# Gated delta rule in a 256-token, four-layer forward pass: forward substitution on 16-row blocks instead of 32-row blocks, and the doubling steps woven by hand into the last gate projection

## The chip, the cores and the metric

One NeuronCore of a Trainium2 chip runs the whole program; the other cores are idle. The metric is the device time of one execution in microseconds (us), lower is better. The profile names the engines PE (TensorE matmuls), PEld (its weight loads), DVE (VectorE), ACT (ScalarE), POOL (GpSimd) and SP (SyncE, which here only issues DMAs).

## The reference

Four layers over 256 tokens of width 1024, all in fp32: MLA attention, MoBA attention, a gated-delta-rule (GDN) layer and a forgetting-attention (FoX) layer; the first two each carry an MLP. The change touches the GDN layer alone. Per head and per chunk of 64 tokens it solves a unit lower triangular system:

```
a_mat = jnp.where(strict, jnp.einsum('bhncd,bhnsd->bhncs', kb, kc) * decay, 0.0)
rhs = jnp.concatenate([vc * bc[..., None], kb * jnp.exp(gcum)[..., None]], axis=-1)
sol = lax.linalg.triangular_solve(a_mat, rhs, left_side=True, lower=True, unit_diagonal=True)
...
def step(S, inp):
    v_new = u_i - jnp.einsum('bhck,bhkv->bhcv', w_i, S)
    o = (jnp.einsum('bhck,bhkv->bhcv', q_i * jnp.exp(g_i)[..., None], S)
         + jnp.einsum('bhcs,bhsv->bhcv', attn_i, v_new))
    S = S * jnp.exp(g_last)[..., None, None] + jnp.einsum('bhck,bhcv->bhkv', k_dec, v_new)
...
o = rms_norm_2(o, o_norm) * jax.nn.silu(z.reshape(B, L, H, GDN_DV))
return o.reshape(B, L, W) @ w_out
```

## The kernel before

Activations live in SBUF with tokens or features on the 128 partitions. Matmuls that must keep fp32 accuracy are made of three fp32r products of split operands (`mm3`, lines 173 to 176: hi*hi, lo*hi, hi*lo); a weight tile of 128x1024 comes by a DMA on SP's queue into `raw`, is copied to `whi` on ScalarE (line 166) and its rest is formed as `wlo` on VectorE (line 167), each in a ring of four buffers. Small squares are multiplied as plain fp32. A scheduler orders the instructions of each engine from their order in the source, their dependencies and a planner's costs; `queued(after)` and `tc.issue_after` add an ordering by hand. PSUM has eight tiles of 128x512: four named `acc` and four named `aux`.

The GDN layer works in chunks of 128 tokens (two, `t`) for 8 heads: 16 units `u`, each with a 128x128 triangular matrix, kept transposed in `NT_`. Its stages, in the order of the source:

- projections with a short convolution for keys, queries and values, two heads at a time (`conv`, lines 930 to 944), each followed one step later by `keys`, `queries` or `values`. `values` (line 1064) transposes the values of a pair on TensorE; its pairs are named values(0) to values(3) below.
- `system`, after the last keys: the four 32x32 diagonal blocks of each of the 16 units go through DRAM (`n_d`) so that each of the 64 blocks lies on a partition of its own, in two halves (128 partitions). GpSimd inverts them by substitution: 31 steps of two elementwise instructions (lines 1008 and 1010).
- `spread`: the inverted blocks go through DRAM (`x_d`, line 1019) back to rows (line 1023), and `place` copies them on ScalarE (line 1030) into `X`, the block diagonal inverse. `spread_T` (line 1036) transposes `X` into `X[:, 1]`, four units (a quad) at a time.
- `grow`: two doubling steps, 32 to 64 and 64 to 128 rows. For each quad, `grow_a` (line 1074) multiplies `NT_` with `X` and VectorE masks the product into `t1`; `grow_b` (line 1089) multiplies `t1` with `X` (at 32 also its transposed twin) and VectorE subtracts (line 1091).
- `gate(1, ...)`: the second half of the output gate, 48 fp32r products of 512 columns between the last projections and the doubling. values(3) is placed between its halves (`between`).
- then `solve` (line 1153), `state`, `correct`, `output` and the output projection.

Of the kernel before, what the change touches and what calls it, by code (L numbers as in the profile page):

```python
# [10 lines left out]
F32 = mybir.dt.float32  # L11
# [47 lines left out]
def layout(inputs):  # L59
# [16 lines left out]
    for s in (32, 64):  # L76
        b = i // s
        cols[f"off{s}"] = ((b[:, None] == b[None, :] + 1) & (b[:, None] % 2 == 1)).astype(np.float64)
# [18 lines left out]
    eye = np.zeros((P, 32, 16), np.float32)  # L97
    for p in range(P):
        for c in range(16):
            eye[p, 2 * c + p // 64, c] = 1.0  # L100
# [10 lines left out]
def kernel(ctx: ExitStack, tc: tile.TileContext, I: dict, out: bass.AP, small_at: dict):  # L111
# [61 lines left out]
    def mm3(o, l, r, start, stop):  # L173
        T.matmul(o, lhsT=l[0], rhs=r[0], start=start, stop=False)  # L174
        T.matmul(o, lhsT=l[0], rhs=r[1], start=False, stop=False)  # L175
        T.matmul(o, lhsT=l[1], rhs=r[0], start=False, stop=stop)  # L176
# [123 lines left out]
    def proj_tok(hT, w, c0, n, between=None):  # L300
# [536 lines left out]
    def gdn():  # L837
# [25 lines left out]
        def gate(q4, h_T, scale, between=None):  # L863

            a = proj_tok(h_T, w, 3 * D + 512 * q4, 512, between)
            for t in range(NT):
# [6 lines left out]
                G.tensor_tensor(zs, zs, C["gdn_o_norm_2"][:, None, :].to_broadcast([P, 4, P]), op=ALU.mult)  # L873
# [52 lines left out]
        behind = []  # L926

        def conv(part, hp):
# [15 lines left out]
            behind[0:1] = [A.activation(dst, y, AF.Silu).ins]  # L944
# [397 lines left out]
```

## Time and profile before

| | |
|---|---|
| median of 3 runs | 953.02 us (951.78 to 958.95) |
| the profiled execution | 948.23 us |
| its span, first to last instruction | 946.4 us |
| mean granted TensorE clock | 0.988 |
| busy: PE / PEld / DVE / ACT / POOL | 95% / 80% / 69% / 56% / 15% |
| GDN layer's last products to its solve | 704.47 to 751.17 us |

In timeline rows the columns are: start, duration, engine, source line, operation, output<-inputs, shape, count, and in brackets the idle time of the engine just before and what ended it. An fp32 matmul of 128x128 has two records in such a row, a transpose one. Times of the profile are from the span's start.

### The profile page before, as it was taken

How to read it: one execution, taken by the hardware profiler on the slowest of the kernel's cores; microseconds unless marked ns; L12 is line 12 of the kernel's file. 1: busy time of each engine (PE TensorE's matmuls, PEld its weight loads, DVE VectorE, ACT ScalarE, POOL GpSimd, SP SyncE). 2: the span in 40 equal slices, each digit the busy share in tenths (PEclk: the TensorE clock that was granted, in tenths of full speed). 3: DMA queues.
4: the chain of work that ended last, by engine and by line, in shares of the span. 5: the costliest groups of instructions: out<-in, count | busy, mean ns of one | idle time of the engine just before them, and what ended most of it. 6: DMA issues, size and time to landing. Idle time of an engine off the chain costs nothing. (4 is left out here: it accounts for less than half of the span.)

```text
span 946.4 us, 13774 instructions
## 1 busy us (share of the span) xinstructions
PE 895.7 (95%) x4962; PEld 756.7 (80%) x4962; DVE 655.8 (69%) x1399; ACT 529.1 (56%) x1001; POOL 144.1 (15%) x190
## 2 busy tenths in 40 slices
PE   8899889999999999999999999999994998998995
PEld 7676678888888878777888888889994986887884
DVE  5997476767665666658566656679982788767775
ACT  6885365655554656555555445489654136755652
POOL 1121123233222100031000000010487000000000
PEclk9999999999999999999999999999997999999998
DMA  8546147777777854437666666355752115456331
GB/s 279 162 134 200 45 157 233 201 207 220 211 207 208 188 162 145 155 91 234 192 197 190 204 199 187 81 173 154 197 168 77 46 47 181 138 171 195 118 111 67
DMA packets 97300, 154.55 MB, mean 163 GB/s; under 512 B 10840, under 2 KB 65920, under 8 KB 96976
## 3 DMA queue, kind: packets, MB, share of 16 engines
q1 hardware_dynamic: 87072, 141.53, 47.8%
q0 software_dynamic: 10016, 12.11, 6.3%
q8 instruction: 39, 0.64, 0.3%
q14 instruction: 29, 0.24, 0.1%
q10 hardware_dynamic: 144, 0.03, 0.0%
HBM read 147.84 MB, written 5.78 MB: 162 GB/s over the span
## 5 line engine op out<-in xcount | busy, mean ns | idle before, releaser
L167 DVE TENSOR_TENSOR wlo<-raw,whi 128x1024 fp32r<-128x1024 f32 (+3 forms) x198 | 239.8, 1214 | 142.1 <-ACT whi L166 140.8
L166 ACT ACTIVATE whi<-raw 128x1024 fp32r<-128x1024 f32 (+3 forms) x202 | 205.9, 1025 | 151.4 <-DMA raw<-in_mlp_w_in_dram 79.6
L679 PE MATMUL aux<-s,whi 128*128 128x512 f32 x512 | 182.3, 399 | 2.7 <-DVE s L260 2.3
L174 PE MATMUL acc<-whi,s 128*128 128x512 f32 (+2 forms) x408 | 160.5, 398 | 5.0 <-ACT whi L166 2.4
L175 PE MATMUL acc<-wlo,s 128*128 128x512 f32 (+2 forms) x408 | 158.8, 391 | 0.8 <-DVE wlo L167 0.8
L176 PE MATMUL acc<-whi,s 128*128 128x512 f32 (+2 forms) x408 | 157.3, 387 | 0.0
L680 PE MATMUL aux<-s,wlo 128*128 128x256 f32 x512 | 143.9, 281 | 2.7 <-DVE wlo L167 2.7
L679 PEld LDWEIGHTS aux<-s,whi 128*128 128x128 f32 x512 | 96.2, 188 | 26.7 <-DVE s L260 2.8
L680 PEld LDWEIGHTS aux<-s,wlo 128*128 128x128 f32 x512 | 96.7, 189 | 4.5 <-DVE wlo L167 3.4
L174 PE MATMUL acc<-s,w2k 128*128 128x512 f32 x256 | 99.9, 390 | 0.0
L175 PE MATMUL acc<-s,w2k 128*128 128x512 f32 x256 | 99.8, 390 | 0.0
L176 PE MATMUL acc<-s,w2k 128*128 128x512 f32 x256 | 99.6, 389 | 0.0
L174 PEld LDWEIGHTS acc<-whi,s 128*128 128x128 f32 x408 | 76.5, 188 | 22.9 <-ACT whi L166 3.5
L175 PEld LDWEIGHTS acc<-wlo,s 128*128 128x128 f32 x408 | 76.8, 188 | 15.1 <-DVE wlo L167 3.1
L176 PEld LDWEIGHTS acc<-whi,s 128*128 128x128 f32 x408 | 76.9, 189 | 13.9 <-issue 0.3
L167 DVE TENSOR_TENSOR s<-raw,s 128x1024 fp32r<-128x1024 f32 x64 | 75.8, 1220 | 8.3 <-ACT s L166 8.1
L166 ACT ACTIVATE s<-raw 128x1024 fp32r<-128x1024 f32 x68 | 68.3, 1048 | 14.1 <-PE acc L176 6.8
L176 PE MATMUL acc<-s,wlo 128*128 128x256 f32 x256 | 72.6, 285 | 3.1 <-DVE wlo L167 3.1
L175 PE MATMUL acc<-s,whi 128*128 128x256 f32 x256 | 73.0, 286 | 0.5 <-DVE s L260 0.2
L174 PE MATMUL acc<-s,whi 128*128 128x256 f32 x256 | 72.9, 285 | 0.4 <-ACT s L259 0.2
L441 POOL DMA_DIRECT2D bias_d<-s x64 | 48.3, 969 | 130.0 <-ACT s L435 111.4
L176 PEld LDWEIGHTS acc<-s,w2k 128*128 128x128 f32 x256 | 48.1, 188 | 10.2
(365 smaller groups left out, 1423.7 us busy)
## 6 DMA issues: line engine op xcount, KB each, us to landing
raw<-in_mlp_w_in_dram SPq DMA_DIRECT2D x64, 512.0 KB, 5.2
raw<-in_mlp_w_out_dram SPq DMA_DIRECT2D x64, 512.0 KB, 3.9
raw<-in_gdn_w_in_dram SPq DMA_DIRECT2D x32, 512.0 KB, 4.4
raw<-in_moba_w_qkv_dram SPq DMA_DIRECT2D x24, 512.0 KB, 4.4
raw<-in_fox_w_in_dram SPq DMA_DIRECT2D x16, 512.0 KB, 5.0
raw<-in_kv_w_dram SPq DMA_DIRECT2D x16, 512.0 KB, 3.8
raw<-in_mla_w_o_dram SPq DMA_DIRECT2D x8, 512.0 KB, 3.6
bias_d<-s POOLq DMA_DIRECT2D x64, 64.0 KB, 4.7
```

Of the source, the lines that this page charges most:

```text
L166: i = A.activation(hi[:, :k * b], rs, AF.Copy)
L167: j = e.tensor_tensor(lo[:, :k * b], rs, hi[:, :k * b].bitcast(F32), op=ALU.subtract)
L174: T.matmul(o, lhsT=l[0], rhs=r[0], start=start, stop=False)
L175: T.matmul(o, lhsT=l[0], rhs=r[1], start=False, stop=False)
L176: T.matmul(o, lhsT=l[1], rhs=r[0], start=False, stop=stop)
L441: nc.gpsimd.dma_start(bias_d[q0:q0 + 8].rearrange("g h k -> h g k"), stg[r0:r0 + 8], accum_op=ALU.add if part else ALU.bypass)
L679: T.matmul(pj[j], lhsT=w[0], rhs=hT[k].rearrange("p a b -> p (a b)"), start=k == 0, stop=False)
L680: T.matmul(pj[j][:, 0:S], lhsT=w[1], rhs=hT[k][:, 0], start=False, stop=k == KD - 1)
```

## The change

Substitution now runs on 16-row diagonal blocks: 128 blocks, one on each partition, 15 steps instead of 31. A third doubling step, 16 to 32 rows, is added (with a third mask, so that the table `small` grows by 128 columns). `spread` writes `x_d` by one DMA and reads it straight into `X` by eight DMAs of 16 rows instead of four into a staging tile; `place` is gone. `grow_b` makes only the product that it updates (`X[:, 0]`, or at 64 `X[:, 1]`) and no transposed twin; instead `spread_T` is done anew before each doubling step, so three times in all. It takes its PSUM tile from `acc` instead of `aux`.

The doubling is written out as one list, `chain`, of 37 steps, each a quad's four TensorE instructions: 4 spread_T, 4 grow_a(16), values(3), 4 grow_b(16), 4 pairs of spread_T and grow_a(32), 4 grow_b(32), 4 pairs of spread_T and grow_a(64), 4 grow_b(64). The first 22 are put among the 16 groups of three products of gate(1) (`weave`: before group 0 one step, and so on), each ordered after the one before; the other 15 follow. The GpSimd multiplications by `egb`, which were ordered after the last DMA of `spread`, are ordered after the last GpSimd multiplication of gate(1).

```diff
--- before.py
+++ after.py
-    for s in (32, 64):
+    for s in (16, 32, 64):
...
+    def proj_tok(hT, w, c0, n, between=None, weave=()):
+
+
+        weave, last = list(weave), []
         a = [acc_tile() for _ in range(NT)]
         for c in range(2):
             wc = load_w(w[:, 4 * c:4 * c + 4, c0:c0 + n], 4, n)
             for t in range(NT):
                 for kk in range(4):
                     k = 4 * c + kk
-                    mm3(a[t][:, :n], sl(hT, slice(None), k, slice(t * P, (t + 1) * P)), wc[kk],
-                        k == 0, k == KD - 1)
+                    if weave:
+                        with queued(last):
+                            last = [weave.pop(0)()]
+                    with queued(last):
+                        last = [mm3(a[t][:, :n], sl(hT, slice(None), k, slice(t * P, (t + 1) * P)), wc[kk],
+                                    k == 0, k == KD - 1)]
...
-        bt = inv[:, 0:1024].rearrange("p (j i) -> p j i", j=32)
-        xb = inv[:, 1024:1536].rearrange("p (i c) -> p i c", i=32)
-        t3 = inv[:, 1536:2048].rearrange("p (i c) -> p i c", i=32)
+        bt = inv[:, 0:256].rearrange("p (j i) -> p j i", j=16)
+        xb = inv[:, 256:512].rearrange("p (i c) -> p i c", i=16)
+        t3 = inv[:, 512:768].rearrange("p (i c) -> p i c", i=16)
...
-            for ch in range(2):
-                nc.gpsimd.dma_start(bt[64 * ch:64 * ch + 64], n_d.rearrange("b u j i -> (b u) j i"))
+            for d in range(2):
+                ds = slice(16 * d, 16 * d + 16)
+                nc.gpsimd.dma_start(bt[64 * d:64 * d + 64], n_d[:, :, ds, ds].rearrange("b u j i -> (b u) j i"))
             nc.gpsimd.dma_start(xb, I["eye"])
-            for i in range(31):
+            for i in range(15):
                 substitute(i)
 
         def substitute(j):
 
-            c, n = j // 2 + 1, 31 - j
+            c, n = j + 1, 15 - j
             G.tensor_tensor(t3[:, 0:n, 0:c], xb[:, j, 0:c][:, None, :].to_broadcast([P, n, c]),
-                            bt[:, j, j + 1:32][:, :, None].to_broadcast([P, n, c]), op=ALU.mult)
-            G.tensor_tensor(xb[:, j + 1:32, 0:c], xb[:, j + 1:32, 0:c], t3[:, 0:n, 0:c], op=ALU.subtract)
+                            bt[:, j, j + 1:16][:, :, None].to_broadcast([P, n, c]), op=ALU.mult)
+            G.tensor_tensor(xb[:, j + 1:16, 0:c], xb[:, j + 1:16, 0:c], t3[:, 0:n, 0:c], op=ALU.subtract)
...
-            x_d = dr.tile([4, 2, 16, 32, 16], F32, tag="x_d", name="x_d")
-            for h in range(2):
-                nc.gpsimd.dma_start(x_d[:, h], xb[64 * h:64 * h + 64])
-            stg = inv[:, 0:512].rearrange("p (h u c) -> p h u c", h=2, u=16)
-            for b in range(4):
-                bs = slice(32 * b, 32 * b + 32)
-                last = nc.gpsimd.dma_start(stg[bs], x_d[b].rearrange("h u i c -> i (h u) c"))
-            return stg, last
-
-        def place(stg):
-            for b in range(4):
-                bs = slice(32 * b, 32 * b + 32)
-                o = X[bs, 0, :, bs].rearrange("p u (c h) -> p h u c", h=2)
-                A.activation(o, stg[bs], AF.Copy)
-
...
-        def spread_T():
-            for u4 in range(4):
-                p = aux_tile()
-                for j in range(4):
-                    T.transpose(p[:, j * P:(j + 1) * P], X[:, 0, 4 * u4 + j], ident)
-                A.activation(X[:, 1, 4 * u4:4 * u4 + 4], p.rearrange("p (a b) -> p a b", a=4), AF.Copy)
+            x_d = dr.tile([2, 4, 16, 16, 16], F32, tag="x_d", name="x_d")
+            nc.gpsimd.dma_start(x_d.rearrange("d b u i c -> (d b u) i c"), xb)
+            for d in range(2):
+                for b in range(4):
+                    bs = slice(32 * b + 16 * d, 32 * b + 16 * d + 16)
+                    last = nc.gpsimd.dma_start(X[bs, 0, :, bs], x_d[d, b].rearrange("u i c -> i u c"))
+            return last
+
+        def spread_T(u4):
+            p = aux_tile()
+            for j in range(4):
+                i = T.transpose(p[:, j * P:(j + 1) * P], X[:, 0, 4 * u4 + j], ident)
+            A.activation(X[:, 1, 4 * u4:4 * u4 + 4], p.rearrange("p (a b) -> p a b", a=4), AF.Copy)
+            return i.ins
...
-                T.matmul(p[:, j * P:(j + 1) * P], lhsT=NT_[:, 4 * u4 + j], rhs=X[:, 0, 4 * u4 + j], start=True, stop=True)
-            t1 = w2k([P, 4, P])
-            V.tensor_tensor(t1, p.rearrange("p (a b) -> p a b", a=4), C[f"off{s}"][:, None, :].to_broadcast([P, 4, P]),
+                i = T.matmul(p[:, j * P:(j + 1) * P], lhsT=NT_[:, 4 * u4 + j], rhs=X[:, 0, 4 * u4 + j], start=True, stop=True)
+            t1[u4] = w2k([P, 4, P])
+            V.tensor_tensor(t1[u4], p.rearrange("p (a b) -> p a b", a=4), C[f"off{s}"][:, None, :].to_broadcast([P, 4, P]),
                             op=ALU.mult)
-            return t1
-
-        def grow_b(s, u4, t1):
+            return i.ins
+
+        def grow_b(s, u4):
+
             us = slice(4 * u4, 4 * u4 + 4)
-            px = {}
-            for z in ((0, 1) if s < 64 else (1,)):
-                px[z] = aux_tile()
-                for j in range(4):
-                    a, b = X[:, 1, 4 * u4 + j], t1[:, j]
-                    if z:
-                        a, b = b, a
-                    T.matmul(px[z][:, j * P:(j + 1) * P], lhsT=a, rhs=b, start=True, stop=True)
-            for z in px:
-                V.tensor_tensor(X[:, z, us], X[:, z, us], px[z].rearrange("p (a b) -> p a b", a=4), op=ALU.subtract)
-
-        def grow():
-            pend = []
-            for s in (32, 64):
-                for u4 in range(4):
-                    pend.append((s, u4, grow_a(s, u4)))
-                    if len(pend) > 1:
-                        grow_b(*pend.pop(0))
-            grow_b(*pend.pop(0))
+            z = int(s == 64)
+            px = acc_tile()
+            for j in range(4):
+                a, b = X[:, 1, 4 * u4 + j], t1[u4][:, j]
+                if z:
+                    a, b = b, a
+                i = T.matmul(px[:, j * P:(j + 1) * P], lhsT=a, rhs=b, start=True, stop=True)
+            V.tensor_tensor(X[:, z, us], X[:, z, us], px.rearrange("p (a b) -> p a b", a=4), op=ALU.subtract)
+            return i.ins
...
-        stg, last = spread()
+        spread()
         f, i, y = pend.pop(0)
-        gate(1, hT, None, lambda: f(i, y))
-        with queued(behind + split):
-            place(stg)
-        spread_T()
-        grow()
...
+        quad = lambda e, *s: [(e, *s, u) for u in range(4)]
+        with_T = lambda s: [g for u in range(4) for g in ((spread_T, u), (grow_a, s, u))]
+        chain = quad(spread_T) + quad(grow_a, 16) + [(f, i, y)] + quad(grow_b, 16) + with_T(32) + quad(grow_b, 32) \
+            + with_T(64) + quad(grow_b, 64)
+        done = []
+
+        def step(n):
+            for _ in range(n):
+                e, *args = chain.pop(0)
+                with queued(done):
+                    done[:] = [e(*args)]
+            return done[0]
+
+        last = gate(1, hT, None, None, [lambda n=n: step(n) for n in (1, 1, 2, 1, 1, 1, 1, 1, 1, 1, 2, 2, 2, 2, 2, 1)])
+        step(len(chain))
...
-        with tc.issue_after(last.ins):
+        with tc.issue_after(last):
             G.tensor_tensor(kT[:, :, P:S], kT[:, :, P:S], egb, op=ALU.mult)
```

TensorE, from the last product of the last convolution. Before, where `s_5823` is the activation of the gate:

```order
L175 MATMUL acc<-s_5824,whi 128x256
L176 MATMUL acc<-s_5823,wlo 128x256
L174 MATMUL acc<-whi,s_5823 128x512
L175 MATMUL acc<-wlo,s_5823 128x512
L176 MATMUL acc<-whi,s_5824 128x512
```

After, where L1060 is values(2), L1031 is `spread_T`, `s_5941` is `X` and L171 to L173 are `mm3`:

```order
L172 MATMUL acc<-s_5824,whi 128x256
L173 MATMUL acc<-s_5823,wlo 128x256
L1060 MATMUL aux<-gains,w2k 128x128 x4
L1031 MATMUL aux<-gains,s_5941 128x128 x4
L171 MATMUL acc<-whi,s_5823 128x512
L172 MATMUL acc<-wlo,s_5823 128x512
L173 MATMUL acc<-whi,s_5824 128x512
```

values(2) stood after the tenth gate product and now stands, with the first quad of `spread_T`, ahead of all of them.

TensorE at the end of the gate. Before, where L1036 is `spread_T`, L1074 `grow_a` and L1089 `grow_b`:

```order
L174 MATMUL acc<-whi,s_5823 128x512
L175 MATMUL acc<-wlo,s_5823 128x512
L176 MATMUL acc<-whi,s_5824 128x512
L1036 MATMUL aux<-gains,s_5941 128x128 x16
L1074 MATMUL aux<-s_5941,s_5933 128x128 x8
L1089 MATMUL aux<-w2k,s_5941 128x128 x4
L1089 MATMUL aux<-s_5941,w2k 128x128 x4
```

After, where L1072 is `grow_a` and L1087 `grow_b`:

```order
L1087 MATMUL acc<-w2k,s_5941 128x128 x4
L171 MATMUL acc<-whi,s_5823 128x512
L172 MATMUL acc<-wlo,s_5823 128x512
L173 MATMUL acc<-whi,s_5824 128x512
L1087 MATMUL acc<-w2k,s_5941 128x128 x12
L1031 MATMUL aux<-gains,s_5941 128x128 x4
L1072 MATMUL aux<-s_5941,s_5933 128x128 x4
```

The whole chain stood behind the last gate product; now its last 15 steps do.

GpSimd at the end of the substitution. Before, where L1124 and L1125 multiply by `egb`, L873 is the gate's multiplication and L794 the next load:

```order
L1010 TENSOR_TENSOR s_5940<-s_5940 128x16
L1019 DMA x_d<-s_5940 4x16x512 x2
L1023 DMA s_5940<-x_d 32x32x16 x4
L1124 TENSOR_TENSOR s_5931<-s_5931,s_5905 128x8x128
L1125 TENSOR_TENSOR s_5930<-s_5930,s_5905 128x8x128
L873 TENSOR_TENSOR s_5739<-s_5739,small 128x512 x2
```

After, with the same three at L1125, L1126 and L876:

```order
L1013 TENSOR_TENSOR s_5940<-s_5940 128x15
L1021 DMA x_d<-s_5940 128x256
L1025 DMA s_5941<-x_d 16x16x16 x8
L876 TENSOR_TENSOR s_5739<-s_5739,small 128x512 x2
L1125 TENSOR_TENSOR s_5931<-s_5931,s_5905 128x8x128
L1126 TENSOR_TENSOR s_5930<-s_5930,s_5905 128x8x128
```

The gate's multiplications now stand ahead of those by `egb`.

The scheduler also orders the FoX layer a little differently. VectorE there, before, where L1247 ends the forget gate, L1253 copies its running sum, L1286 is the gate of a head pair and L1266 builds the decay bias from a row that comes back from DRAM:

```order
L1247 TENSOR_TENSOR gsp<-gm,gsp 128x16
L167 TENSOR_TENSOR wlo<-raw,whi 128x1024
L1253 COPY cc<-aux 128x16
L167 TENSOR_TENSOR wlo<-raw,whi 128x1024 x2
L1286 TENSOR_TENSOR w2k<-acc,w1k 128x512
L1266 SCALAR_TENSOR_TENSOR s_7998<-s_7996,cc,small 128x128
```

After:

```order
L1248 TENSOR_TENSOR gsp<-gm,gsp 128x16
L1254 COPY cc<-aux 128x16
L164 TENSOR_TENSOR wlo<-raw,whi 128x1024 x2
L1267 SCALAR_TENSOR_TENSOR s_8041<-s_8039,cc,small 128x128
```

One weight split and one gate instruction moved from ahead of the decay bias to behind it.

## Rows read from the trace of the kernel before

**Rows 1.** The page's second part: the clock in 40 slices.

```profile
PEclk9999999999999999999999999999997999999998
```

**Rows 2.** Waits of TensorE, whole span: total, times, longest (us).

```profile
PE aux L1036 <- ACT s L1030: 12.3, 1, 12.3
...
PE acc L176 <- DVE wlo L167: 3.1, 1, 3.1
PE acc L176 <- DVE s L260: 2.8, 1, 2.8
```

**Rows 3.** Timeline of TensorE, the gate to the solve.

```profile
704.47 0.40 PE L174 MATMUL acc<-whi,s 128*128 128x512 f32 x1
...
706.77 0.60 PE L1064 MATMUL aux<-gains,w2k 128*128 128x128 f32 x4
...
707.67 0.40 PE L174 MATMUL acc<-whi,s 128*128 128x512 f32 x1
...
714.49 0.39 PE L174 MATMUL acc<-whi,s 128*128 128x512 f32 x1
...
729.09 3.68 PE L1036 MATMUL aux<-gains,s 128*128 128x128 f32 x16 [12.29 <-ACT s L1030]
732.55 2.33 PE L1074 MATMUL aux<-s,s 128*128 128x128 f32 x16
...
741.19 1.06 PE L1089 MATMUL aux<-s,w2k 128*128 128x128 f32 x8
...
751.17 1.95 PE L1153 MATMUL aux<-s,s 128*128 128x128 f32 x16
```

**Rows 4.** Timeline of GpSimd, the substitution and what follows it.

```profile
671.77 1.08 POOL L1000 DMA_DIRECT2D s<-n_d  x2 [2.41 <-DMA n_d<-s]
678.86 0.25 POOL L1008 TENSOR_TENSOR s<-s 128x31 f32<-128x31 f32 x1 [6.01 <-DMA s<-n_d]
...
679.57 1.10 POOL L1008 TENSOR_TENSOR s<-s 128x30 f32<-128x30 f32 x1
...
716.87 1.32 POOL L1019 DMA_DIRECT2D x_d<-s  x2 [0.30 <-POOL s L1010]
723.13 3.14 POOL L1023 DMA_DIRECT2D s<-x_d  x4 [4.94 <-issue]
...
730.90 3.13 POOL L873 TENSOR_TENSOR s<-s,small 128x512 f32<-128x512 f32 x2
```

**Rows 5.** Line 1023 alone: its DMAs' issue times (ns) and landings.

```profile
L1023 POOL DMA_DIRECT2D s<-x_d x4: 789/794/804, 723.1 to 725.5; - x4
...
DMA to landing us min/median/max: 2.8/2.9/3.0
```

**Rows 6.** Timeline of ScalarE around the start of the gate.

```profile
704.55 1.06 ACT L166 ACTIVATE whi<-raw 128x1024 fp32r<-128x1024 f32 x1 [0.38 <-PE acc L175]
706.00 0.63 ACT L944 ACTIVATE w2k<-w2k 128x512 f32<-128x512 f32 x1 [0.39 <-DVE w2k L941]
```

**Rows 7.** Timeline of TensorE, a run of transposes in the FoX layer.

```profile
836.25 1.92 PE L748 MATMUL aux<-gains,s 128*128 128x128 f32 x16
838.01 0.61 PE L788 MATMUL aux<-gains,rn 128*128 128x128 f32 x4
```

**Rows 8.** Stretches: us, busy of PE, PEld, DVE, ACT, POOL, PEclk, DMA share, GB/s.

```profile
729.00:732.60 3.60, 3.52 (x17) 3.52 (x18) 1.83 (x1) 3.26 (x6) 3.60 (x3) 0.50 0.00 0
...
734.90:740.00 5.10, 5.10 (x46) 5.10 (x47) 4.71 (x7) 0.00 (x0) 0.00 (x0) 1.00 0.53 184
...
795.00:796.00 1.00, 0.65 (x2) 0.38 (x2) 0.40 (x3) 0.84 (x4) 0.00 (x0) 0.50 1.05 377
...
855.00:856.00 1.00, 1.00 (x11) 1.00 (x10) 1.00 (x2) 0.00 (x0) 0.00 (x0) 1.00 0.42 94
```

**Rows 9.** Timeline of VectorE, then of TensorE, in the FoX layer.

```profile
847.41 5.36 DVE L1266 SCALAR_TENSOR_TENSOR s<-s,cc,small 128x128 f32<-128x128 f32 x16 [2.86 <-DMA s<-cr_d]
...
854.56 0.39 PE L176 MATMUL acc<-s,wlo 128*128 128x256 f32 x1 [3.06 <-DVE wlo L167]
```

More of the change, by code (lines that the diff above doesn't have):

```diff
@@ L95, in layout @@
                            np.broadcast_to(pos[None, :], (P, S))], axis=1)
[L97 to L100, printed above, removed]
+    eye = np.ascontiguousarray(np.broadcast_to(np.eye(16, dtype=np.float32), (P, 16, 16)))
     arrays = {
@@ L175, in mm3 @@
         T.matmul(o, lhsT=l[0], rhs=r[1], start=False, stop=False)
-        T.matmul(o, lhsT=l[1], rhs=r[0], start=False, stop=stop)
+        return T.matmul(o, lhsT=l[1], rhs=r[0], start=False, stop=stop).ins
     def sl(pair, *idx):
@@ L298, in wview @@
         return w.rearrange("(k p) n -> p k n", p=P)
-    def proj_tok(hT, w, c0, n, between=None):
+    def proj_tok(hT, w, c0, n, between=None, weave=()):
+        weave, last = list(weave), []
         a = [acc_tile() for _ in range(NT)]
@@ L861, in ab_rows, with gate @@
                 V.tensor_scalar(ab[:, t], p[:, 16 * t:16 * t + 16], rn[:, t:t + 1], None, op0=ALU.mult)
-        def gate(q4, h_T, scale, between=None):
-            a = proj_tok(h_T, w, 3 * D + 512 * q4, 512, between)
+        def gate(q4, h_T, scale, between=None, weave=()):
+            a = proj_tok(h_T, w, 3 * D + 512 * q4, 512, between, weave)
             for t in range(NT):
@@ L872, in gate @@
                     A.activation(zs, z4, AF.Silu, scale=scale[:, t:t + 1])
-                G.tensor_tensor(zs, zs, C["gdn_o_norm_2"][:, None, :].to_broadcast([P, 4, P]), op=ALU.mult)
+                i = G.tensor_tensor(zs, zs, C["gdn_o_norm_2"][:, None, :].to_broadcast([P, 4, P]), op=ALU.mult)
+            return i.ins
         gate(0, hT0, rn, ab_rows)
@@ L924, in gdn @@
         vt = slot(7, [P, NT, H, P])
-        behind = []
         def conv(part, hp):
@@ L943, in conv @@
             dst = (qT, kT)[part][:, 2 * hp:2 * hp + 2, :] if part < 2 else w2k([P, 2, S])
-            behind[0:1] = [A.activation(dst, y, AF.Silu).ins]
+            A.activation(dst, y, AF.Silu)
             return dst
@@ L1063, in values @@
                 for t in range(NT):
-                    T.transpose(p[:, (2 * t + j) * P:(2 * t + j + 1) * P], vT[:, j, t * P:(t + 1) * P], ident)
+                    k = T.transpose(p[:, (2 * t + j) * P:(2 * t + j + 1) * P], vT[:, j, t * P:(t + 1) * P], ident)
             for t in range(NT):
-                i = V.tensor_tensor(vt[:, t, hs], p[:, 256 * t:256 * t + 256].rearrange("p (a b) -> p a b", a=2),
+                V.tensor_tensor(vt[:, t, hs], p[:, 256 * t:256 * t + 256].rearrange("p (a b) -> p a b", a=2),
                                     rki[:, t, hs, None].to_broadcast([P, 2, P]), op=ALU.mult)
-            behind[1:] = [i.ins]
+            return k.ins
+        t1 = {}
         def grow_a(s, u4):
@@ L1073, in grow_a @@
             for j in range(4):
-                T.matmul(p[:, j * P:(j + 1) * P], lhsT=NT_[:, 4 * u4 + j], rhs=X[:, 0, 4 * u4 + j], start=True, stop=True)
-            t1 = w2k([P, 4, P])
-            V.tensor_tensor(t1, p.rearrange("p (a b) -> p a b", a=4), C[f"off{s}"][:, None, :].to_broadcast([P, 4, P]),
+                i = T.matmul(p[:, j * P:(j + 1) * P], lhsT=NT_[:, 4 * u4 + j], rhs=X[:, 0, 4 * u4 + j], start=True, stop=True)
+            t1[u4] = w2k([P, 4, P])
+            V.tensor_tensor(t1[u4], p.rearrange("p (a b) -> p a b", a=4), C[f"off{s}"][:, None, :].to_broadcast([P, 4, P]),
                             op=ALU.mult)
-            return t1
-        def grow_b(s, u4, t1):
+            return i.ins
+        def grow_b(s, u4):
             us = slice(4 * u4, 4 * u4 + 4)
-            px = {}
-            for z in ((0, 1) if s < 64 else (1,)):
-                px[z] = aux_tile()
-                for j in range(4):
-                    a, b = X[:, 1, 4 * u4 + j], t1[:, j]
-                    if z:
-                        a, b = b, a
-                    T.matmul(px[z][:, j * P:(j + 1) * P], lhsT=a, rhs=b, start=True, stop=True)
-            for z in px:
-                V.tensor_tensor(X[:, z, us], X[:, z, us], px[z].rearrange("p (a b) -> p a b", a=4), op=ALU.subtract)
-        def grow():
-            pend = []
-            for s in (32, 64):
-                for u4 in range(4):
-                    pend.append((s, u4, grow_a(s, u4)))
-                    if len(pend) > 1:
-                        grow_b(*pend.pop(0))
-            grow_b(*pend.pop(0))
+            z = int(s == 64)
[6 more added lines that the diff above has]
+            V.tensor_tensor(X[:, z, us], X[:, z, us], px.rearrange("p (a b) -> p a b", a=4), op=ALU.subtract)
+            return i.ins
         pend = []
```

## The prediction, made before the changed kernel ran

> **What bounds the kernel now.** I read the page's slices first: TensorE's clock is at 9 in all slices but the last (8) and one inside, 709.8 to 733.5 us, which shows 7 [rows 1]. The table of TensorE's waits says why: the longest wait of the span, 12.3 us, is for one line, 1036, the first `spread_T`; the next two are 3.1 and 2.8 us [rows 2]. So one place is worth a change of this size, and I read its timelines. On TensorE [rows 3] the gate's products start at 704.47 us, the wait of 12.29 ends at 729.09, the solve starts at 751.17: 46.70 us. GpSimd [rows 4] shows who is late: substitution from 678.86 to 716.58 (62 instructions), then the write of `x_d`, the read back issued from 723.13, ScalarE's copies, and only then TensorE. The clock is the second loss: 0.50 from 729.0 to 732.6, 1.00 from 734.9 on [rows 8]. Sixteen transposes took 3.46 us there (729.09 to 732.55) against 1.76 at full clock (836.25 to 838.01) [rows 3, 7].
>
> **When X is there.** The read of the blocks issued at 671.77 moved 256 KB per DMA and let the substitution start at 678.86 [rows 4]. Now each of the two moves 1024 pieces of 64 bytes, as many as a DMA of line 1023, which took 0.79 us to issue and 2.9 to land [rows 5]: 671.77 + 0.79 + 2.9 + 0.65 (the same delay as before between landing and first instruction) = 676.1; 678.86 is the other end. The substitution has 30 instructions instead of 62. An undisturbed small one takes 0.25 to 0.35 us with a gap of 0.08; eleven of the 62 took some 0.93 us more, as the one at 679.57 (1.10 against 0.25 for the neighbour of the same size) [rows 4]. 30 x 0.37 = 11.1, and 5 such delays make 15.8; the ends are 11.1 (no delay) and 18.2 (the old mean, 37.7/62, though the old ones are larger). So `xb` is done at 691.9, between 687.2 and 697.1. From the last subtraction (716.58) to the first read back took 6.55 us with two writes of 0.66 each [rows 4]; with one, 5.9. Eight read issues of at most 0.79 (each has a quarter of the pieces) put the last 5.5 later, and it lands 2.9 after that and is seen 0.2 later [rows 5]. X: 691.9 + 5.9 + 5.5 + 3.1 = 706.4, between 701.7 and 711.6. The four copies of `place` are gone.
>
> Before it lands, TensorE stands at values(2), which is now ahead of all gate products. Its input, the silu of line 944, ran from 706.00 because ScalarE first had to make a split that waits for the buffers of the last convolution [rows 6]; nothing of that moves. So values(2) starts at 706.77 as before, TensorE idles 2.3 us from 704.47 (in the kernel before, gate products covered that), and spread_T can start at 707.2. X is, by 0.8 us, not the last to arrive: I take 707.2.
>
> **The path from there, on TensorE.** Gate products: 48; thirty of them from 707.67 to 714.49 go at 0.227 us [rows 3], so 10.9. Transposes: twelve quads of spread_T and values(3) at 0.44 (1.76/4) [rows 7], 5.7. Doubling products: 12 quads of grow_a and 12 of grow_b; the eleven quads from 741.19 to 751.17 went at 0.907 each with all their waits [rows 3], so 21.8. A product behind foreign work is some 0.09 later than in a row of its own kind (values(2) at 706.77 and two products fill the 0.90 us to 707.67, 0.44 + 0.45): 16 times, 1.5. Sum 39.9; with 2.3 and 0.44 for values(2), 42.6 against 46.70: **4.1 us less**.
>
> As a balance: removed are the wait (12.3), the half clock (1.7 on the transposes, 0.5 on the first products) and 0.5 of short waits inside the gate; added are eight quads of transposes (3.5), four of grow_a (3.6), the switches (1.5) and the wait for values(2) (2.3). What is saved on GpSimd is mostly paid back on TensorE, since at full clock the doubling is bound by TensorE, not by its latencies.
>
> **What is woven behind what.** ScalarE now copies out the first two spread_T quads ahead of the second half of the last convolution, and VectorE does the four masks ahead of the splits of the output weights. I followed both queues with the durations that these operations have in this stretch (0.6 us for a copy, 0.7 for a mask or subtraction, 1.1 + 1.2 for a split): values(3) has its input some 5 us after the start of the chain and is reached after 11; the fourth mask of step 32, behind a split that waits for gate group 13, is done 3.0 us after that group and needed after 5.4. So these cost nothing; if a split were 2.4 us late, it would be 1 to 2 us. GpSimd's multiplication by `egb` now stands behind the gate's, which took 3.13 for two [rows 4] and waits for the last silu at about 736; with 2.4 us for each of the two it ends near 742, ahead of `correct` at about 751. 64 KB more of `small` at the start: under 0.3 us.
>
> **The FoX layer.** There the forget gate's matmuls move seven gate products ahead and the decay bias one split ahead. The bias (5.36 us on VectorE) waits for a DMA at 847.41, and TensorE waits 3.06 us for the split behind it, to 854.56 [rows 9]. By the same queue reckoning the DMA lands some 2 us earlier, while the split that TensorE then lacks is an earlier one (it needs it 1.8 us earlier): between 1 us better and 1 us worse; I take zero.
>
> **Rivals.** (A) Faster by more: the delays in the substitution don't matter and the FoX order gives its 1 us, the switches cost nothing (1.5): about 6.5 us less. Against it, the PE sum has little air.
>
> (B) The clock falls in the new idle time. The rows say both: after the 2.8 us wait it was 0.50 at 795 us, after the 3.1 us one it was 1.00 at 855 [rows 2, 8]. Products at half clock cost some 2 us in the stretch of 729 to 733 [rows 3]: a gain of about 2.
> [...]
>
> (C) X is late and TensorE waits for it: slower. Every microsecond after 707.2 is one lost, so from 711.3 on the change loses. By the sum's upper end, 711.6, with the clock falling again (2 us), it is 2.3 us slower. If the eight reads went one after the other at 2.9 us, X would come at 691.9 + 5.9 + 23.2 = 721.0, 13.8 after 707.2: with the clock, 11.7 slower. Against it: the four of line 1023, issued 0.79 apart, each landed 2.8 to 3.0 after their own issue [rows 5], so they overlap.
> The Trainium skill, "DMA: Bandwidth & Descriptors" (section on the SWDGE path), gives each such DMA about 2 us of fixed cost, and its section on bandwidth calls transfers under 64 KB bound by descriptors; by that, eight of 16 KB are the wrong way, and eight fixed costs in a row would be 16 us (an estimate from that page), X at 713.8 and the kernel 2.5 slower. The rows of line 1023 speak for overlap instead.
>
> (D) The change doesn't do what it says, the chain staying behind the gate: not so, the order of TensorE's instructions shows it woven.
>
> **How the numbers follow.** The profiled execution took 948.23, 1.8 more than its span, and lies 4.8 below the median of 953.02. In its own terms the forecast is 948.2 - 4.1 = 944.1; against the median, 948.9, so 949. Chances: forecast 0.55, A 0.12 (946.5), B 0.18 (951), C 0.15 (955.3, with a tail to 965). The runs before spread over 7 us, so a median of three may be off by 3. The range, 944 to 955, holds the forecast, A and B with most of that spread, and the nearer half of C; it leaves out the tail of C. About 1% (9.5 us) is what a measurement of this kernel can tell from no change: faster by more than that 0.09, within it 0.83, slower 0.08.
>
> **What would show it.** Right: the wait for line 1036 gone and nothing over 3 us in its place; X's last DMA landing before 707; solve starting at about 747; clock 1.00 from 700 to 751; FoX stage within 1 us. Wrong, if spread_T's first quad waits for a DMA past 711, if grow_b waits for VectorE inside the weave, or if the clock shows 0.50 behind values(2).

## The result, and the profile after

The changed kernel took 943.52 us (median of 4 runs, 941.28 to 950.12) against 954.02 for the kernel before (4 runs, 951.78 to 958.95): ratio 0.9904, 95% interval 0.9879 to 0.9930. Measured again beside three of the experiments it took 947.1 (6 runs) against 954.11: 0.9928, 0.9905 to 0.9951. So it is faster, by the ratios some 7 to 9 us; 4 had been forecast.

The profiled execution after took 941.28 us, its span 939.5, which is 6.9 less than before. I split this difference at two anchors that both traces have. *The stretch* runs from the end of the last convolution product (its start and 0.12 us, the pace of these products) to the start of the solve; *the tail* from there to the end of the span.

| profiled execution | start of the stretch | stretch | tail | span |
|---|---|---|---|---|
| before | 704.47 | 46.7 | 195.2 | 946.4 |
| after | 705.74 | 40.9 | 192.9 | 939.5 |
| difference | +1.3 | -5.8 | -2.3 | -6.9 |

The first row of differences is noise: the start of the stretch lies between 704.5 and 711.0 in all the profiles of this study, though TensorE's program up to there is the same (the last section says what moves it).

TensorE's clock by slices, after, and then the table of its waits over the whole span (columns: engine and line, releaser, us in total, times, longest), to be read against [rows 1] and [rows 2]:

```profile
PEclk9999999999999999999999999999999999999998
```

```profile
engine line waited for: us in total, times, longest us
...
PE acc L173 <- DVE s L257: 2.8, 1, 2.8
...
PE aux L1060 <- ACT w2k L946: 2.0, 1, 2.0
...
PE acc L173 <- DVE wlo L164: 1.6, 2, 0.8
```

The wait of 12.3 us for `spread_T` is gone, the 7 in the clock's row too. New is 2.0 us for values(2) (now line 1060). The wait of 3.1 in [rows 2], for the split of weights behind the FoX bias, is now 0.8.

TensorE's timeline of the stretch (start, us, operation), against [rows 3]:

```profile
705.62 0.28 PE L173 MATMUL acc<-s,wlo 128*128 128x256 f32 x1
707.87 0.66 PE L1060 MATMUL aux<-gains,w2k 128*128 128x128 f32 x4 [1.97 <-ACT w2k L946]
708.36 0.60 PE L1031 MATMUL aux<-gains,s 128*128 128x128 f32 x4
708.72 0.48 PE L171 MATMUL acc<-whi,s 128*128 128x512 f32 x1
...
712.20 1.06 PE L1072 MATMUL aux<-s,s 128*128 128x128 f32 x8
713.01 0.48 PE L171 MATMUL acc<-whi,s 128*128 128x512 f32 x1
...
743.03 3.74 PE L1087 MATMUL acc<-s,w2k 128*128 128x128 f32 x32
746.60 1.61 PE L1154 MATMUL aux<-s,s 128*128 128x128 f32 x13
```

`spread_T` starts at 708.36 and waits for nothing; a doubling quad inside the weave occupies 0.81 (712.20 to 713.01), and the product behind it 0.32 instead of 0.23; the last four quads take 0.89 each (3.57/4). GpSimd's timeline, against [rows 4], and the last of the eight reads of X show that X is only just in time:

```profile
673.08 0.83 POOL L1003 DMA_DIRECT2D s<-n_d  x1 [2.32 <-DMA n_d<-s]
...
679.78 0.21 POOL L1011 TENSOR_TENSOR s<-s 128x15 f32<-128x15 f32 x1 [4.60 <-DMA s<-n_d]
...
680.71 1.30 POOL L1013 TENSOR_TENSOR s<-s 128x28 f32<-128x28 f32 x1
...
692.80 1.23 POOL L1011 TENSOR_TENSOR s<-s 128x15 f32<-128x15 f32 x1
694.11 0.22 POOL L1013 TENSOR_TENSOR s<-s 128x15 f32<-128x15 f32 x1
694.63 0.61 POOL L1021 DMA_DIRECT2D x_d<-s  x1 [0.30 <-POOL s L1013]
698.70 4.46 POOL L1025 DMA_DIRECT2D s<-x_d  x8 [3.46 <-DMA x_d<-s]
```

```profile
L1025 POOL DMA_DIRECT2D s<-x_d x1: 562/562/562, 702.6 to 702.6; - x1
...
DMA to landing us min/median/max: 4.8/4.8/4.8
```

The substitution takes 14.55 us (679.78 to 694.33), the eight reads are issued in 4.46, and the last one, issued at 702.6, lands at 707.4: 0.9 us before `spread_T` starts. In the FoX layer (VectorE, then TensorE's wait) the bias now runs 838.64 to 844.0 and the split behind it is only just late, against [rows 9]:

```profile
838.64 5.36 DVE L1267 SCALAR_TENSOR_TENSOR s<-s,cc,small 128x128 f32<-128x128 f32 x16 [2.98 <-DMA s<-cr_d]
...
844.51 1.22 DVE L164 TENSOR_TENSOR wlo<-raw,whi 128x1024 fp32r<-128x1024 f32 x1
```

```profile
845.78 0.39 PE L173 MATMUL acc<-s,wlo 128*128 128x256 f32 x1 [0.83 <-DVE wlo L164]
```

### The profile page after: what moved, and what is told of

Its sections match the earlier page's. It is cut to its first block, busy times and chain, and to the rows that moved or that the text cites. A ratio compares the mean times of both kernels' runs of the same rounds, so it can differ in the third digit from the quotient of the medians.

```text
span 939.5 us, 13905 instructions
## 1 busy us (share of the span) xinstructions
PE 901.8 (96%) x5026; PEld 763.3 (81%) x5026; DVE 654.8 (70%) x1403; ACT 529.4 (56%) x1005; POOL 123.3 (13%) x161
## 3 DMA queue, kind: packets, MB, share of 16 engines
HBM read 147.25 MB, written 5.65 MB: 163 GB/s over the span
## 4 chain that ended last, share of the span: by engine, by line
PE 60%; DVE 13%; DMA 13%; ACT 7%; issue 6%; POOL 0%; DVEq 0%; ACTq 0%; POOLq 0%; SPq 0%
PE acc L173 13%; PE acc L171 13%; PE acc L172 13%; DMA raw<-in_mlp_w_in_dram 9%; PE aux L682 6%; DVE wlo L164 4%; ACT whi L163 3%; PE aux L683 3%; DVE s L164 2%; DMA raw<-in_moba_w_qkv_dram 1%; PE acc L1087 1%; PE aux L1072 1%; PE aux L374 1%; PE aux L378 1%; PE aux L646 1%
## 5 line engine op out<-in xcount | busy, mean ns | idle before, releaser
L171 PE MATMUL acc<-whi,s 128*128 128x512 f32 (+2 forms) x408 | 162.3, 402 | 4.1 <-ACT s L604 1.7
L173 PE MATMUL acc<-whi,s 128*128 128x512 f32 (+2 forms) x408 | 158.5, 390 | 0.0
L682 PEld LDWEIGHTS aux<-s,whi 128*128 128x128 f32 x512 | 96.2, 188 | 27.2 <-DVE s L257 2.8
L171 PE MATMUL acc<-s,w2k 128*128 128x512 f32 x256 | 100.0, 391 | 0.1
L173 PE MATMUL acc<-s,w2k 128*128 128x512 f32 x256 | 99.8, 390 | 0.0
L171 PEld LDWEIGHTS acc<-whi,s 128*128 128x128 f32 x408 | 76.9, 189 | 20.9 <-ACT s L604 2.1
L173 PEld LDWEIGHTS acc<-whi,s 128*128 128x128 f32 x408 | 77.5, 190 | 13.9 <-DVE s L1301 0.3
L173 PE MATMUL acc<-s,wlo 128*128 128x256 f32 x256 | 72.8, 286 | 1.6 <-DVE wlo L164 1.6
L171 PE MATMUL acc<-s,whi 128*128 128x256 f32 x256 | 73.0, 285 | 0.4 <-ACT s L256 0.3
L173 PEld LDWEIGHTS acc<-s,w2k 128*128 128x128 f32 x256 | 48.1, 188 | 10.6 <-DVE w2k L702 0.4
```

The costliest lines, as they stand in the source:

```text
L173: return T.matmul(o, lhsT=l[1], rhs=r[0], start=False, stop=stop).ins
L682: T.matmul(pj[j], lhsT=w[0], rhs=hT[k].rearrange("p a b -> p (a b)"), start=k == 0, stop=False)
```

## The experiments

The theory to be tested (W): the early X removes a wait of TensorE, and from there the stretch is TensorE's own work, so that neither the weaving nor a still earlier X gives anything. Rivals: the weaving hides latencies of the chain (L); X still arrives last (X); and, for the tail, that its 2.3 us are jitter (N) and not the order in the FoX layer (F). All nine runs (the two named "X early" leave out most of the substitution's steps, so their X is only partly computed and they serve for timing alone):

| kernel | stretch | TensorE's wait in it | tail | wait for a split there | ratio to before, 95% |
|---|---|---|---|---|---|
| changed, again | 42.5 | 2.0 values(2) | 192.3 | 0.2 | 0.9928 (0.9905 to 0.9951) |
| not woven | 38.65 | none | 192.8 | 1.0 | 0.9875 (0.9851 to 0.9899) |
| values(2) behind products | 38.8 | none | 193.4 | 1.2 | 0.9867 (0.9837 to 0.9897) |
| X delayed | 50.0 | 2.3 values(2), 6.5 X | 193.6 | 0.7 | single run, 950.3 us |
| X early | 40.9 | 2.0 values(2) | 195.1 | 2.3 | single run, 942.9 us |
| FoX bias late | 40.9 | 2.0 values(2) | 199.4 | 5.7 | 0.9992 (0.9970 to 1.0013) |
| before, X early | 33.4 | 0.8 and 0.2 | 195.0 | 2.9 | single run, 940.8 us |
| before, FoX order | 46.0 | 11.6 X | 193.0 | 0.3 | 0.9962 (0.9932 to 0.9993) |
| not woven, bias in parts | 38.6 | none | 191.3 | none | 0.9873 (0.9843 to 0.9904) |

### The changed kernel again

No edit.

> The changed kernel again, as the base for the other three runs of this job. If the gain of the first result (9 to 10 us) is real, this run is 0.988 to 0.993 of the kernel before. In the profile the stretch from the last convolution product to the solve takes 40.9 us again (46.7 before) and the stretch from the solve to the end 192.9 (195.2 before), each within 0.5 us.

The ratio is as expected, the stretch is not: 42.5. The wait for values(2) is the same 1.97 us to the hundredth, but here the clock fell behind it. Windows of the first profile after, then of this one (columns: window, its length, TensorE busy, granted clock, DMA):

```profile
706.00:708.00 2.00, 0.13 (x1) 1.00 0.26 49
...
710.00:712.00 2.00, 2.00 (x15) 1.00 0.71 236
```

```profile
708.70:711.00 2.30, 0.33 (x4) 1.00 0.33 82
711.00:712.00 1.00, 1.00 (x7) 0.64 0.92 311
712.00:714.00 2.00, 2.00 (x8) 0.50 0.85 266
714.00:716.00 2.00, 2.00 (x14) 0.83 0.17 70
```

So rival B of the prediction happens in some executions: with the same wait the clock stayed at 1.00 in three profiles (after, X early, FoX bias late) and fell to 0.50 in one, where it cost 1.6 us. How often it falls in executions without a profile is not shown.

### Not woven

```
-        last = gate(1, hT, None, None, [lambda n=n: step(n) for n in (1, 1, 2, ...)])
+        last = gate(1, hT, None, lambda: f(i, y))
+        done[:] = gate_last          # the gate's last product
         step(len(chain))             # chain without values of the last pair
```

> Blocks of 16 rows as in the changed kernel, but the doubling steps all stand behind the gate's last product, and values of the last pair between the gate's halves, as before the change. Theory W (TensorE's own work bounds the stretch, so the weaving in itself is worth nothing, and the early X is all of the gain): 48 products x 0.227 + 2 values quads and 12 spread_T quads x 0.44 + 24 doubling quads x 0.89 = 38.4, and the 2.0 us wait for values(2) is filled by gate products: 38.4 to 40 from the last convolution product to the solve, 1 to 2.5 us less than woven (40.9). Rival L (a doubling step alone waits for masks, subtractions and copies, which the weaving hides): each of the three steps has 1 us or more of waits on TensorE behind VectorE or ScalarE, the stretch is 43 or more and the kernel 2 us or more slower than the changed one.

38.65 against 38.4 worked out, no wait at all in the stretch, and the kernel is about 5 us faster than the woven one measured beside it. TensorE's timeline of the chain:

```profile
722.93 1.91 PE L1031 MATMUL aux<-gains,s 128*128 128x128 f32 x16
724.68 3.73 PE L1072 MATMUL aux<-s,s 128*128 128x128 f32 x32
728.25 3.74 PE L1087 MATMUL acc<-w2k,s 128*128 128x128 f32 x32
...
746.05 3.74 PE L1087 MATMUL acc<-s,w2k 128*128 128x128 f32 x32
749.62 1.95 PE L1155 MATMUL aux<-s,s 128*128 128x128 f32 x16
```

Four transposing quads follow each other in 1.75 us, four doubling quads in 3.57, without a gap: with four quads in each step, masks, subtractions and copies are done while TensorE is at the other three. Rival L falls; the whole gain of the stretch is the early X. Here `spread_T` needs X only at 722.93, and the last read landed at 710.75, so that this order also leaves X 12 us in hand where the woven one leaves 1.

The stretch explains 2.2 to 3.8 of the 5 us (40.9 or 42.5 against 38.65). The rest may lie with the clock: its granted mean over an execution was 0.986 to 0.990 in the six of the woven kernel and 0.989 to 0.995 in the six of this one. Where it fell in the executions without a profile is not shown.

### Values(2) behind the first products

```
-                    f(i, y)
+                    if (f, i) == (values, H // 2 - 2):
+                        early = (f, i, y); continue      # becomes chain[0]
+                    f(i, y)
-for n in (1, 1, 2, 1, 1, 1, 1, 1, 1, 1, 2, 2, 2, 2, 2, 1)
+for n in (None, None, None, 2, 2, 2, 2, 1, 1, 2, 2, 2, 2, 2, 2, 2)
```

> The changed kernel, but values(2) and the whole chain stand behind the gate's first three groups of products (3 x 3 x 0.227 = 2.0 us). Theory W: the wait of 2.0 us for values(2) is filled, X has landed by then, and nothing takes its place: the stretch to the solve 38.9 instead of 40.9, the kernel 2 us faster than the changed one (ratio to the kernel before lower by 0.002). Rival X (the last reads of X land about when values(2) ends, so that the wait only changes its name): spread_T waits for a DMA and the stretch stays at 40 or more.

38.8: the wait is filled and nothing takes its place.

```profile
706.83 0.28 PE L173 MATMUL acc<-s,wlo 128*128 128x256 f32 x1
706.95 0.40 PE L171 MATMUL acc<-whi,s 128*128 128x512 f32 x1
...
709.07 0.66 PE L1062 MATMUL aux<-gains,w2k 128*128 128x128 f32 x4
...
745.72 1.50 PE L1159 MATMUL aux<-s,s 128*128 128x128 f32 x12
```

Woven without the wait (38.8) and not woven (38.65) are equal to 0.15 us: switching between kinds of products costs nothing, and the weaving's own effect was the idle time in front of it. (The last read of X landed at 705.90 here.)

### X delayed, X early

```
             for i in range(15):
                 substitute(i)
+            for _ in range(16):
+                G.tensor_tensor(t3, xb, bt, op=ALU.mult)
```

> The changed kernel with 16 more products of GpSimd (128x256 each, their result unused) between the last subtraction and the write of x_d. At 0.5 to 0.65 us each X lands 8 to 10 us later. Theory W, with rival C of the prediction as its other side (every microsecond after spread_T's turn is lost): the last read of X lands some 2.3 us ahead of the first spread_T now, so TensorE waits 5.5 to 8 us more in front of it, the clock falls to 0.50 behind that wait, and the stretch to the solve is 47 to 50.5 instead of 40.7. Rival S (X has been there long before, and the slack is 8 us or more): the stretch stays under 43.

50.0, as theory W has it. Here `spread_T` is what waits, and the products behind it run at half clock (0.57 and 0.43 between starts, where 0.31 and 0.23 are usual):

```profile
707.40 0.66 PE L1062 MATMUL aux<-gains,w2k 128*128 128x128 f32 x4 [2.27 <-ACT w2k L946]
714.61 1.09 PE L1033 MATMUL aux<-gains,s 128*128 128x128 f32 x4 [6.55 <-DMA s<-x_d]
715.35 0.78 PE L171 MATMUL acc<-whi,s 128*128 128x512 f32 x1
715.92 0.63 PE L172 MATMUL acc<-wlo,s 128*128 128x512 f32 x1
716.35 0.63 PE L173 MATMUL acc<-whi,s 128*128 128x512 f32 x1
```

The added products delay the reads of X and not its write: they only read `xb`, as the write does, and the write was issued at 694.19, ahead of fifteen of them. The last read was issued 9.6 us later than after the change (712.2 against 702.6), but landed 2.0 us after its issue instead of 4.8, at 714.2 against 707.4, and `spread_T` started 0.5 after that. So in the first profile after the change X landed 0.9 us ahead of `spread_T`, of which that half microsecond has to be taken; in the second profile it was 1.2, in the one with the FoX bias late 6.3. Rival C of the prediction is real as a mechanism, and its point was less than 1 us away.

```
-            for i in range(15):
+            for i in range(0, 15, 3):
```

> The changed kernel with 5 of the 15 steps of the substitution (the other ten are left out, so X is only partly computed): X lands some 9 us earlier. Theory W (X is not the last to arrive, values(2) is): the wait of 2.0 us for values(2) stays and the stretch to the solve is 40.7, or 42.3 where the clock falls behind that wait. Rival X (X arrives last or holds buffers that something else waits for): the stretch is 39 or less.

40.9, with the same 2.0 us for values(2). X some 13 us earlier (reads issued from 685.83, against 698.70; the last landed at 693.8) changes nothing in the stretch. The tail of this profile is 195.1, no shorter than before the change, with a wait of 2.3 us for the split in the FoX layer; the section on that layer comes back to it.

### The kernel before with an early X

```
-            for i in range(31):
+            for i in range(0, 31, 6):
```

> The kernel before with 6 of the 31 steps of its substitution (25 are left out, so X is only partly computed): its X, of blocks of 32 rows, is there long before the gate ends. Shows what the wait of 12.3 us is worth if nothing is paid for its removal. Theory W: 48 products x 0.227 + 2 values quads and 4 spread_T quads x 0.44 + 20 doubling quads x 0.91 = 31.7 from the last convolution product to the solve, 31.5 to 33 (46.5 with the wait), so that blocks of 16 rows cost 6 to 7 us of TensorE's time against it (8 quads of transposes, 4 of grow_a). Rival L (the doubling steps wait for other engines once the clock is up): 35 or more.

33.4, of which 1.0 are waits for ScalarE's copies (0.77 and 0.22); the sum had 31.7 without any. Against the 38.65 of the kernel that was not woven, blocks of 16 rows cost TensorE 5 to 6 us. The span fell only to 939.0 because something new happened ahead of the stretch: TensorE waited 4.5 us for values(1), since one split of VectorE took 5.65 us. VectorE's row and GpSimd's:

```profile
697.25 5.65 DVE L167 TENSOR_TENSOR wlo<-raw,whi 128x1024 fp32r<-128x1024 f32 x1 [0.31 <-ACT whi L166]
```

```profile
697.10 2.42 POOL L1124 TENSOR_TENSOR s<-s,s 128x1024 f32<-128x1024 f32 x1
699.45 2.35 POOL L1125 TENSOR_TENSOR s<-s,s 128x1024 f32<-128x1024 f32 x1
```

It ended 1.1 us after GpSimd's two multiplications, started while the first was running, and takes 1.22 otherwise (last section).

### The order in the FoX layer

In the changed kernel, the transposes of the decay sums, the way through memory and the bias are held back behind the first 24 products of the first gate pair:

```
                 for j in range(2):
                     i = proj_T(hTq, wc, j, ...)
+                    if (hp, j) == (0, 0):
+                        with queued([i]):
+                            bias()     # transposes of cc, cr_d, db
```

> The changed kernel, with one edit in the FoX layer alone: the transposes of the decay sums, the DMA through memory and the bias stand behind the first half (24 products) of the first FoX gate pair, near where they stood before the change (10 products in). Theory F (2.3 us of the gain come from the order that the scheduler gave the FoX layer, and not from the delta rule): TensorE's wait there for a split of weights, 0.8 in the changed kernel, is 3 us or more again, and the stretch from the solve to the end is 195 to 197 instead of 192.9; the stretch up to the solve stays at 40.9. Rival N (that 2.3 is jitter of loads between executions): the end stretch stays within 0.7 us of 192.9.

The tail is 199.4, more than theory F had: the bias waits until 854.14 for its DMA, the split behind it ends at 861, TensorE waits 5.7 us, and the clock is 0.50 from 858 to 864. The stretch is 40.9 as before the edit. The change's whole gain is lost with this one edit (0.9992). It holds the bias back further than the kernel before did (24 products instead of 10), so it shows that this order can cost as much, not how much of the change's gain came from it.

```profile
854.14 5.35 DVE L1270 SCALAR_TENSOR_TENSOR s<-s,cc,small 128x128 f32<-128x128 f32 x16 [8.45 <-DMA s<-cr_d]
...
860.01 1.21 DVE L164 TENSOR_TENSOR wlo<-raw,whi 128x1024 fp32r<-128x1024 f32 x1
```

The other way round, in the kernel before the gate's products are put behind the transposes of the decay sums:

```
+                with queued([first]):      # first: the second transpose of cc
                     for j in range(2):
                         proj_T(hTq, wc, j, o[:, j * S:(j + 1) * S])
```

> The kernel before with one edit in the FoX layer alone: the products of the FoX gate stand behind the transposes of the decay sums (10 of them stood ahead), so that the bias starts some 1.2 us earlier. Theory F (the order in the FoX layer gives time of its own, whatever the delta rule does): TensorE's wait for the split, 3.1, falls to 1 to 2, the stretch from the solve to the end is 193 to 194.5 instead of 195.2, and the kernel 0.997 to 0.999 of the one before. Rival N: the transposes themselves make TensorE wait for VectorE's copy, and nothing is won: 195 or more.

The tail is 193.0 and the wait for the split 0.3: this one edit alone makes the kernel before 3.6 us faster (0.9962; the interval reaches from 0.7 to 6.5 us), 2.2 of it visible in the tail. Rival N's cost is there, but it is 0.4 us (TensorE's wait for the copy of the sums).

```profile
852.13 0.39 PE L176 MATMUL acc<-s,wlo 128*128 128x256 f32 x1 [0.27 <-DVE wlo L167]
```

What the order does is to be read on GpSimd, which issues the write of the decay sums to memory and the read back; before the change, then after it:

```profile
837.12 0.55 POOL L1260 DMA_DIRECT2D cr_d<-w1k  x1 [70.34 <-ACT w1k L1258]
842.73 0.57 POOL L1262 DMA_DIRECT2D s<-cr_d  x1 [5.06 <-DMA cr_d<-w1k]
```

```profile
830.64 0.57 POOL L1261 DMA_DIRECT2D cr_d<-w1k  x1 [68.71 <-ACT w1k L1259]
833.06 0.57 POOL L1263 DMA_DIRECT2D s<-cr_d  x1 [1.86 <-PE aux L791]
```

Counted from the solve the write is issued 1.9 us earlier (84.0 against 86.0). It also lands sooner: 5.0 us after its issue before the change and 4.6 in the one other profile with the old order, 1.6 to 1.9 in the six with the changed kernel's order, 2.5 with the edit above. Why it lands sooner is open. The read back takes 4.6 and 4.8 us in the old order and 4.7 to 7.1 in the new, the 7.1 in the profile with X early, and there the wait for the split is 2.3. So rival N has a share: the six tails of the new order lie between 192.3 and 195.1, their mean is 193.3, and the two of the old order are 195.0 and 195.2. In the mean of these profiles the order is worth some 1.8 us, and in one of the six nothing.

### A kernel that is faster than both

The kernel that was not woven, with the bias in three parts behind the splits of the second to fourth gate pair:

```
                 wc = load_w(wz[:, :, D + hp * 256:D + (hp + 1) * 256], KD, 256)
+                if hp:
+                    with queued(split[1:]):
+                        bias(range(3 * hp - 3, min(3 * hp, H)))
```

> The kernel that was not woven, with one more edit in the FoX layer: the bias (16 instructions on VectorE, 5.4 us) is made in three parts, each behind the splits of the second, third and fourth gate pair, so that no split of weights waits for the whole of it or for its DMA. Theory F (the FoX wait is a split queued behind the bias): TensorE's wait for that split, 0.2 to 1.2 us in the kernels with this order, goes, and the stretch from the solve to the end is 191.5 to 192.6 (192.8 with the bias in one piece); the stretch up to the solve stays at 38.5; the kernel about 0.986 to 0.987 of the one before. Rival A (attention needs the bias at once, and waits for the last part): the wait moves to the first logits' softmax, and the end stretch is 193 or more.

Tail 191.3, stretch 38.6, no wait for a split in the tail. VectorE's timeline shows two splits ahead of the second part of the bias:

```profile
840.41 1.41 DVE L1269 SCALAR_TENSOR_TENSOR s<-s,cc,small 128x128 f32<-128x128 f32 x4 [2.90 <-DMA s<-cr_d]
...
842.99 2.36 DVE L164 TENSOR_TENSOR wlo<-raw,whi 128x1024 fp32r<-128x1024 f32 x2
845.26 2.06 DVE L1269 SCALAR_TENSOR_TENSOR s<-s,cc,small 128x128 f32<-128x128 f32 x6
```

1.5 us in the tail are less than the timing can tell: 0.9873 is the ratio of the kernel that was not woven (0.9875) too. Both, and the one with values(2) moved, are some 5 us faster than the changed kernel.

## Why the prediction was right, and what it missed

The mechanism held: no wait over 3 us took the place of the removed one, and the gain is small because TensorE pays most of it back. The size, 4.1 us, was too small: 5.8 in the stretch and 2.3 in the tail were seen, less 1.6 where the clock falls. The median of the first measurement (943.5) lies half a microsecond below the range, that of the second (947.1) in it. Of the signs that the prediction named, the wait was gone, the solve started at 746.6 and the clock stayed at 1.00 in the first profile; X's last read landed at 707.4 and not before 707, and the FoX stage was 2.3 us off and not within 1.

- **When X is there.** Read to first substitution: 6.7 us (673.08 to 679.78; 4.3 taken, with 7.1 as the other end). Substitution: 14.55 (15.8 taken). To the first read back: 4.4 (5.9 taken). From the first issue to the last: 3.9 (5.5 taken); the last landing 4.8 after its issue (3.1 taken). X at 707.4 against 706.4, `spread_T`'s turn at 708.36 against 707.2: 0.9 us in hand where 0.8 was forecast. Every term was off by 1 us or more and the errors cancelled, so that X was not last by so little a margin is luck as much as reckoning.
- **Values(2).** Forecast 2.3 us idle, measured 1.97. This was the one real cost of the new order, and two orders without it show that it bought nothing: 38.65 and 38.8 instead of 40.9.
- **The sum on TensorE** is the term that was mis-sized: 39.9 from `spread_T` on, measured 38.2 (708.36 to 746.60). The 16 switches at 0.09 (1.5 us) are nothing: woven and not woven differ by 0.15. The row that they were read from [rows 3] says so itself, since 0.44 and 0.45 are 0.89 of its 0.90 us: the first product behind a quad takes 0.08 more, and the quad ahead of it 0.08 less (708.36 to 708.72, 0.36 instead of 0.44). The doubling quads cost 0.89, not 0.907: the last two of the eleven that set the price took 0.97 each.
- **The balance.** Without the wait for X the old blocks would have taken 33.4, the new ones 38.65: blocks of 16 rows cost 5 to 6 us of TensorE's time where 7.1 (3.5 and 3.6) had been put, and remove some 13.
- **FoX taken as zero** is the step that failed: 2.3 us better in the profile. The working had the DMA of the decay sums 2 us earlier and the split needed 1.8 earlier. Counted from the solve, the split was needed 2.0 earlier and the write issued 1.9 earlier, as it had said; but the bias started 4.2 earlier (92.0 against 96.2), since the write landed after 1.8 us instead of 5.0. The working had no term for that, and the wait shrank from 3.06 to 0.83. In six profiles with this order it was 0.2 to 2.3, in two with the old order 2.9 and 3.1. The edit of that layer alone on either kernel shows that the order matters whatever the delta rule does.
- **Rivals.** A was what happened, and by two of the terms that it named: the switches cost nothing and the FoX order gave its 1 us and more. B happens in some executions. C needs X less than 1 us later than in the first profile. The Trainium skill, "DMA: Bandwidth & Descriptors" (section on the SWDGE path), gives each such DMA a fixed cost of about 2 us; the trace disagrees with the estimate that adds up eight of them, 16 us: from the first issue to the last landing the eight reads took 8.7 us (698.7 to 707.4), each landing 2.2 to 4.8 after its own issue.

## What to carry to other kernels

When a long wait is removed by more work on the engine that waited, count that work at the price of a row without waits; the gain is the wait less that. Here a chain of four independent quads in each step hides its own latencies, so weaving it into other products gives nothing and takes the slack from the input that it needs (X at 708 instead of 723). Pulling one late input (here values(2)) ahead of work that is ready costs its whole delay. After any edit under a scheduler, look at stages that were not edited: here the order of a few instructions in another layer was worth some 2 us in one direction and 6 in the other; compare stretches between anchors of one trace, because the absolute start of a stage moved by 6.5 us between executions.

## What the runs showed of the hardware that was not expected

**GpSimd's substitution and VectorE's splits hold each other up.** The delays of some 0.9 us in the substitution, which the prediction took as chance, coincide with VectorE's splits. After the change there are four substitution instructions over 1 us, and four splits in that time, each beginning at most 0.22 us before its partner; VectorE's rows of the first and the last, whose partners on GpSimd (680.71 and 692.80) are shown above:

```profile
680.68 1.22 DVE L164 TENSOR_TENSOR wlo<-raw,whi 128x1024 fp32r<-128x1024 f32 x1
...
692.73 1.23 DVE L164 TENSOR_TENSOR wlo<-raw,whi 128x1024 fp32r<-128x1024 f32 x1 [0.73 <-ACT whi L163]
```

Before, eleven of 62 were long, beside eleven splits. Where the splits fall at other steps, the long instructions move with them: three and three with the FoX bias late, one and one with X early. Of the sixteen products added in the run with X delayed, those that start inside a split take 1.13 to 1.60 us, the others 0.73 to 0.75. With GpSimd first it is VectorE that stands: the split of 5.65 us above. The Trainium skill, "SBUF — State Buffer" (section "SBUF: two separate sides"), says that an operation of VectorE with two inputs in SBUF and one of GpSimd that reads SBUF take a shared port, that whichever starts first has it for the whole instruction, and that the other blocks; the traces agree. No edit was made to test it, so that this is read from which instructions coincide; that the port is the cause is the page's word and not shown here.

**The same idle time can cost the clock or not.** 1.97 us of idle behind the same products left the clock at 1.00 three times and at 0.50 once, for 1.6 us. Not every place is so: a wait of 2.8 us for VectorE, 43 us behind the solve, is in all eleven profiles, and a clock of 0.50 goes with it in all eleven (from 792 to 794 us in the profile after, from 795 to 797 in the one before). Short falls at other places (0.66 from 9 to 14 us in the profile after, 1.00 there in the one before) come and go. From 88 to 101 us the mean granted clock was 0.61 to 0.74 in four profiles (changed again, not woven, FoX bias late, bias in parts) and 1.00 in the other seven; in those four the stretch starts at 708.8 to 711.0. In six of the seven it starts at 704.5 to 707.0, and in the seventh (before, X early) at 710.55, behind its wait of 4.5 us. So most of the movement of that start goes with this one fall.
